# Attention by half blocks: tiles of 2 heads × 64 queries against 192 keys, values' product in six narrow passes

## The chip, the cores and the metric

The kernel runs on one NeuronCore of a Trainium2 chip. The metric is the time of one execution on the device, in microseconds (us). A core has five engines with instruction queues of their own, which run beside each other and wait for each other by semaphores: TensorE (PE, matrix products; the loading of its weights is shown as PEld), VectorE (DVE), ScalarE (ACT), GpSimd (POOL) and SyncE (SP), which here issues every DMA transfer between memory (DRAM) and the on-chip buffers (SBUF). Matrix products land in PSUM, a small memory in eight banks.

## The reference, cut to what matters

One decoder block on 2048 tokens of width 1024: a projection to 7680 columns, a convolution branch, an attention branch, gates, two output projections and norms. The change concerns the attention: 16 query heads and 4 key heads of 64 dimensions, a window of 128 keys, and a sink term in the softmax.

```python
def sliding_window_attention(q, k, v, sinks):
    ...
    qb = q.reshape(B, nb, BLOCK, N_KV_HEADS, GROUP, HEAD_DIM)
    kb, vb = band(k), band(v)                     # previous block and this one: 256 keys
    scores = jnp.einsum("bnqhgd,bnkhd->bnhgqk", qb, kb).astype(jnp.float32) * (HEAD_DIM ** -0.5)
    ...
    rel = qi + BLOCK - kj
    in_window = (rel >= 0) & (rel < WINDOW)       # BLOCK = WINDOW = 128
    ...
    scores = jnp.where(mask[None, :, None, None], scores, jnp.float32(-1e30))
    m = jnp.maximum(jnp.max(scores, axis=-1, keepdims=True), sink)
    p = jnp.exp(scores - m)
    denom = jnp.sum(p, axis=-1, keepdims=True) + jnp.exp(sink - m)
    probs = (p / denom).astype(v.dtype)
    out = jnp.einsum("bnhgqk,bnkhd->bnqhgd", probs, vb)
    return out.reshape(B, S, ATTN_WIDTH)
```

Each query sees exactly 128 keys. Of the 256 that a block of 128 queries is multiplied with, half are masked.

## The kernel before

**Numbers.** Every float32 operand of a large product is split into a high part (rounded to the format that TensorE takes in one pass, F32R) and a low part (the rest). A product is three passes: high·high, high·low, low·high. `put_split` and `split_lo` make the parts, on ACT and on DVE or POOL. The weights' low parts (`wlo`) are computed in the first sweep, stored to memory (`d_lo`), and read back in the second.

**Stages.** There are two sweeps (`s`) of 1024 tokens, each in eight blocks of 128. A sweep projects the GLU inputs, keys, values and queries, then the gates (`mm_ag`, `mm_cg`, `mm_ma`, `mm_mc`), then takes the two output projections (`mm_ya`, `mm_yc`) and the last product (`o`). A projection item is 48 passes of 512 columns, 10.88 us. The convolution runs on DVE (L512), spread over the same stretch.

**Order.** TensorE's order is the order in which the Python code emits its instructions. `Line` keeps a planned time: `project` yields 0.2275 us a pass, and after each step `Line.spend` looks whether a step of a chain is due. Each of the 32 tiles of attention in a sweep (head group `g` of 4 heads, block `b`) is such a chain, `attention(n)`, started every `ATT_EVERY` = 13.8 planned us, in three steps:

1. scores (`sc`, L690): eight passes, 4 heads × 2 key parts, of 256 key columns (128 in the very first block); then the copy to SBUF (L699), the predicated copy of the own block's half (L700), and the softmax (L704 to L715). As each query sees 128 keys, the two key blocks are folded into 128 slots: a slot holds the key of the own block up to the diagonal, and the previous block's after it;
2. after `LAT[0]` = 22 planned us: four transposes (`tpp`, L720) and the split of the result (`pt`, L725 and L248), and on POOL a masked copy of both parts (`pc`, L731);
3. after `LAT[1]` = 16: the values' product (`ov`, L740), four passes of 512 columns: `pt`, high and low, with the previous block's values `vt`, and `pc`, high and low, with the difference of the blocks' values `vd`. The output is scaled by a gate and stored to `d_a`.

`sc` takes two and `tpp` and `ov` one each of three PSUM banks (`tp`), in turn: a tile's scores need the bank that the transposes before them filled, and wait for the split of `pt` (DVE, L248).

Other engines' order, and that of the DMAs on SP, is set by a scheduler from priorities. SP issues in order and a DMA that waits holds up those behind it. In a sweep a round `r` of four projects the queries of one head of each group (`q_a`, `q_b`), rotates them, splits them and stores them to `d_q` (L605), two halves of 512 tokens each; `load_qk` brings a tile's queries and keys (L663, L667).

Of the kernel before, what the change touches and what calls it, by code (L numbers as in the profile page):

```python
# [19 lines left out]
P = 128  # L20
# [27 lines left out]
LAT = (22.0, 16.0)  # L48
# [5 lines left out]
def hybrid_block(ctx: ExitStack, tc: tile.TileContext, x, xt, par_d, w_in, w_conv, sinks, w_attn, w_out,  # L54
# [69 lines left out]
    causal_i = causal.bitcast(I32).unsqueeze(1).broadcast_to([P, 2, P])  # L124
# [7 lines left out]
    def load_sinks():  # L132
        nc.sync.dma_start(out=sink_bc, in_=sinks.partition_broadcast(P).rearrange("p o h -> p (o h)"))
        dve.tensor_scalar(out=nsink, in0=sink_bc, scalar1=-1.0, scalar2=None, op0=ALU.mult)
# [21 lines left out]
    d_q = dram.tile([2, 2, P, S // P, GQ, P], F32, name="d_q")  # L156
    d_k = dram.tile([2, 2, P, S], F32, name="d_k")

    d_a = dram.tile([NSWEEP * KC, P, 2, T], F32, name="d_a")
    v_halo = const.tile([P, NKV, 2, HD], F32R, name="v_halo")  # L160
# [328 lines left out]
    def sweep(s):  # L489
# [84 lines left out]
        def rope_items(name, e, store):  # L574
# [7 lines left out]
            def ev_b(half, ps):  # L582
# [6 lines left out]
                for i in range(2):  # L589
                    hl = slot(next_of("hl", AT[7:11]), [P, 2, TH], F32R, f"hl{s}_{name}_{half}_{i}")  # L590
                    put_split(hl, a[:, i, :], dve)
                    store(i, half, f(hl))
# [4 lines left out]
        def store_k(i, half, hl):  # L597
            t0 = s * T + half * TH
            nc.sync.dma_start(out=d_k[:, i, :, t0:t0 + TH].rearrange("a p t -> p a t"), in_=hl)

        def store_q(r):
            def store(i, half, hl):
                b0 = s * NB + 4 * half
                for a in range(2):
                    nc.sync.dma_start(out=d_q[a, i, :, b0:b0 + 4, r, :],  # L605
                                      in_=hl[:, a, :].rearrange("p (b t) -> p b t", t=P))

            return store


        vt, vd = {}, {}

        def v_item(i):
            def chain(half, vs):
# [8 lines left out]
                act.copy(v_last[:, i], vf[:, 3])  # L623
                for j in range(2):
                    bp = 2 * half + j
                    if i == 0:
                        vt[bp] = slot(AT[bp], [P, 2, NKV, 2 * HD], F32R, f"vt{s}_{bp}")
                        vd[bp] = slot((AT[15:] + X[1:] + X[:1])[bp], [P, 2, NKV, 2 * HD], F32R, f"vd{s}_{bp}")
                    for full, to in ((tp, vt), (d, vd)):
                        part = full[:, 2 * j:2 * j + 2, :].rearrange("p b (g d) -> p b g d", d=HD)  # L630
                        hi, lo = (to[bp][:, :, 2 * i:2 * i + 2, a * HD:(a + 1) * HD] for a in range(2))
                        act.copy(hi, part)
                        split_lo(lo, part, hi, dve)
# [16 lines left out]

        done, qk = {}, {}

        def load_qk(n):
# [5 lines left out]
            q, k = t[:, 0, :].rearrange("p (r t) -> p r t", t=P), t[:, 1, :].rearrange("p (a t) -> p a t", a=2)  # L659
            qk[n] = (q, k)  # L660
            fs = slice(g * HH, (g + 1) * HH)
            for i in range(4):
                nc.sync.dma_start(out=f(q[i * HH:(i + 1) * HH]), in_=d_q[i // 2, i % 2, fs, blk, :, :])  # L663
# [8 lines left out]
        def attention(n):  # L672
# [8 lines left out]
            for h in range(GQ):  # L681
                if h % 2 == 0:
                    scs.append(tp_ps.tile([P, 2, 2, P], F32, tag="tp", name=f"sc{u}_{h // 2}"))
                sc = scs[-1][:, h % 2]
                for j in range(2):
                    if first:
                        o, r = sc[:, 1, :], k[:, j, P:]
                    else:
                        o, r = sc, k[:, j]
                    pe.matmul(out=o, lhsT=q[:, h, :], rhs=r, start=(j == 0), stop=(j == 1))  # L690
# [5 lines left out]
            for i, sc in enumerate(scs):  # L696
                part = sb[:, 2 * i:2 * i + 2, :]
                if not first:
                    act.copy(part, sc[:, :, 0, :])  # L699
                dve.copy_predicated(out=part, mask=causal_i, data=sc[:, :, 1, :])  # L700
# [15 lines left out]
            yield 0.96, LAT[0]  # L716
# [7 lines left out]
            pt = slot(next_of("pt", AT[7:9]), [P, 2, GQ, P], F32R, f"pt{u}")  # L724
            act.copy(pt[:, 0], tpp)  # L725
            split_lo(pt[:, 1], tpp, pt[:, 0], dve)
            if first:
                seq = [(v_of(g, b), pt)]
            else:
                pc = slot(next_of("pc", AT[9:11]), [P, 2, GQ, P], F32R, f"pc{u}")  # L730
                pool.affine_select(out=pc, in_=f(pt), pattern=[[0, 2], [0, GQ], [1, P]],  # L731
                                   compare_op=ALU.is_ge, fill=0.0, base=0, channel_multiplier=-1)
                seq = [(v_of(g, b - 1), pt), (vd[b // 2][:, b % 2, g, :], pc)]
            yield 0.44, LAT[1]

            ov = tp_ps.tile([P, GQ, P], F32, tag="tp", name=f"ov{u}")
            nm = 2 * len(seq)
            for i in range(nm):
                vv, pp = seq[i // 2]
                pe.matmul(out=ov, lhsT=vv, rhs=pp[:, i % 2], start=(i == 0), stop=(i == nm - 1))  # L740
            ovp = ov.rearrange("p (i r) q -> p i r q", r=2)
            for r, own, other in ((0, slice(0, HD), slice(HD, P)), (1, slice(HD, P), slice(0, HD))):
                act.copy(oT[own], ovp[other, :, r, :])
                dve.tensor_tensor(out=oT[own], in0=ovp[own, :, r, :], in1=oT[own], op=ALU.add)
# [10 lines left out]
            yield nm * MM_US, 0.0  # L755

        def start_attention():
            load_qk(0)
            for n in range(NKV * NB):
# [367 lines left out]
```

## Time and profile before

| what | us |
|---|---|
| median of 3 runs | 2013.75 (2013.27 to 2015.22) |
| the profiled execution | 2013.65 |
| its span, first to last instruction | 2011.9 |
| PE busy | 1993.2 |
| DVE / ACT / POOL busy | 1346.4 / 1032.0 / 394.7 |
| mean granted clock of TensorE | 0.999 of full speed |

A row of groups reads: line, engine, operation, out<-in, shape, how often | busy us, mean ns of one | idle time of the engine before it and what ended it. A row of the timeline reads: start, duration, engine, line, operation, how often [idle time before it <- what ended it]; the duration of a matrix product holds its run through the array and overlaps the next, so its pace is seen from starts. A row of waits reads: who <- for whom: us in total, times, longest. A row of stretches reads: from:to, length, then the busy us of PE, PEld, DVE, ACT and POOL with counts, clock, DMA share and GB/s.

### The profile page before, as it was taken

The page shows a single profiled execution, that of the slowest core. Times are in us where ns is not written, and L with a number is a line of the kernel's source. Part 1 is how long each engine was busy: PE and PEld are TensorE (multiplying, and loading weights), DVE is VectorE, ACT ScalarE, POOL GpSimd, SP SyncE. Part 2 cuts the span into 40 slices and gives each one's busy share as a digit, 9 for nine tenths or more (in the row PEclk, how much of TensorE's full clock was granted, in tenths as well). Part 3 has the DMA queues.
Part 4 walks back from the last instruction along what each step waited for, and adds up shares of the span by engine and source line. Part 5 has one row for each costly group of instructions (what it writes and reads, how often), then busy time and mean ns, then how long its engine had stood idle before and what let it go on. Part 6 is the DMA issues. An engine that isn't in the chain of part 4 may idle for free.

```text
span 2011.9 us, 27257 instructions
## 1 busy us (share of the span) xinstructions
PE 1993.2 (99%) x9136; PEld 1655.4 (82%) x9136; DVE 1346.4 (67%) x1934; ACT 1032.0 (51%) x2270; POOL 394.7 (20%) x328
## 2 busy tenths in 40 slices
PE   8999999999999999999999999999999999999998
PEld 7888888887888888888888888888888888888887
DVE  6999679988996265123858669699888824431324
ACT  8322677667777354123523126777777764621222
POOL 0444332333232213241001120111011100001200
PEclk9999999999999999999999999999999999999999
DMA  8445655545556847445634556555545677564422
GB/s 306 147 143 175 225 166 171 166 155 169 168 172 216 263 171 247 146 156 214 218 117 159 160 175 194 166 175 176 175 153 171 181 229 262 175 227 141 157 110 84
DMA packets 268843, 361.13 MB, mean 180 GB/s; under 512 B 28576, under 2 KB 127008, under 8 KB 268704
## 3 DMA queue, kind: packets, MB, share of 16 engines
q1 hardware_dynamic: 268704, 359.40, 54.9%
q8 instruction: 72, 1.18, 0.2%
q14 instruction: 67, 0.55, 0.1%
HBM read 239.75 MB, written 119.54 MB: 179 GB/s over the span
## 4 chain that ended last, share of the span: by engine, by line
PE 88%; DVE 8%; DMA 1%; issue 1%; ACT 1%; SPq 0%; POOL 0%; ACTq 0%; DVEq 0%; POOLq 0%
PE o L1050 9%; PE mm_ya L286 9%; PE mm_yc L286 9%; PE mm_ga L286 8%; PE mm_gb L286 8%; PE mm_mc L286 7%; PE mm_ma L286 7%; PE mm_ag L286 6%; PE mm_cg L286 6%; DVE acc L512 5%; PE mm_q_a L286 4%; PE mm_q_b L286 4%; PE sc L690 2%; PE mm_v L286 2%; PE ov L740 2%
## 5 line engine op out<-in xcount | busy, mean ns | idle before, releaser
L512 DVE SCALAR_TENSOR_TENSOR acc<-glu,par,acc 128x1024 f32<-128x1024 f32 x464 | 595.9, 1284 | 5.9
L1050 PE MATMUL o<-wo,mT 128*128 128x512 f32 x768 | 174.8, 389 | 0.0
L1050 PEld LDWEIGHTS o<-wo,mT 128*128 128x128 f32 x768 | 144.1, 188 | 30.0
L286 PE MATMUL mm_ma<-hT,whi_ma 128*128 128x512 f32 x512 | 159.7, 393 | 0.0
L286 PE MATMUL mm_cg<-hT,whi_cg 128*128 128x512 f32 x512 | 159.7, 393 | 0.0
L286 PE MATMUL mm_ag<-hT,whi_ag 128*128 128x512 f32 x512 | 159.4, 392 | 0.0
L286 PE MATMUL mm_mc<-hT,whi_mc 128*128 128x512 f32 x512 | 157.9, 390 | 0.0
L286 PE MATMUL mm_ya<-aT,whi_ya 128*128 128x512 f32 x512 | 157.7, 389 | 0.0
L286 PE MATMUL mm_yc<-uT,whi_yc 128*128 128x512 f32 x512 | 157.7, 389 | 0.0
L731 POOL TENSOR_SCALAR_AFFINE_SELECT pc<-pt 128x1024 fp32r<-128x1024 f32 x60 | 65.6, 1094 | 431.8 <-DVE pt L248 431.8
L286 PE MATMUL mm_gb<-hT,whi_gb 128*128 128x512 f32 x448 | 139.4, 392 | 0.0
L286 PE MATMUL mm_ga<-hT,whi_ga 128*128 128x512 f32 x448 | 139.3, 392 | 0.0
L286 PEld LDWEIGHTS mm_ya<-aT,whi_ya 128*128 128x128 f32 x512 | 96.1, 188 | 20.0
L286 PEld LDWEIGHTS mm_yc<-uT,whi_yc 128*128 128x128 f32 x512 | 96.1, 188 | 19.9
L286 PEld LDWEIGHTS mm_mc<-hT,whi_mc 128*128 128x128 f32 x512 | 95.9, 188 | 20.0
L286 PEld LDWEIGHTS mm_ag<-hT,whi_ag 128*128 128x128 f32 x512 | 94.3, 188 | 18.4
L286 PEld LDWEIGHTS mm_cg<-hT,whi_cg 128*128 128x128 f32 x512 | 94.0, 188 | 18.2
L286 PEld LDWEIGHTS mm_ma<-hT,whi_ma 128*128 128x128 f32 x512 | 94.0, 188 | 18.1
L710 ACT ACTIVATE ss<-ss,st 128x128 f32<-128x128 f32 x256 | 99.7, 390 | 13.5 <-DVE st L705 12.7
L286 PE MATMUL mm_cg<-hT,wlo_cg 128*128 128x512 f32 x256 | 99.9, 390 | 0.0
L286 PE MATMUL mm_ma<-hT,wlo_ma 128*128 128x512 f32 x256 | 99.9, 390 | 0.0
L286 PE MATMUL mm_ag<-hT,wlo_ag 128*128 128x512 f32 x256 | 99.9, 390 | 0.0
(467 smaller groups left out, 4261.1 us busy)
## 6 DMA issues: line engine op xcount, KB each, us to landing
qk<-d_q SPq DMA_DIRECT2D x256, 64.0 KB, 2.2
d_a<-ss SPq DMA_DIRECT2D x128, 128.0 KB, 1.9
aT<-d_a SPq DMA_DIRECT2D x32, 512.0 KB, 5.7
qk<-d_k SPq DMA_DIRECT2D x240, 64.0 KB, 2.0
raw_ag<-in_w_in_dram SPq DMA_DIRECT2D x32, 256.0 KB, 3.7
d_ag<-ag SPq DMA_DIRECT2D x32, 256.0 KB, 2.2
ss<-d_ag SPq DMA_DIRECT2D x64, 128.0 KB, 2.6
raw_cg<-in_w_in_dram SPq DMA_DIRECT2D x32, 256.0 KB, 3.3
```

The costliest lines, as they stand in the source:

```text
L286: pe.matmul(out=ps, lhsT=a, rhs=b, start=(k == 0 and i == 0), stop=(k == KC - 1 and i == 2))
L512: dve.scalar_tensor_tensor(out=to, in0=glu[c][:, j:j + T], scalar=tap(c, j), in1=acc[c], op0=ALU.mult, op1=ALU.add)
L690: pe.matmul(out=o, lhsT=q[:, h, :], rhs=r, start=(j == 0), stop=(j == 1))
L710: act.activation(out=sb[:, h, :], in_=sb[:, h, :], func=AF.Exp, scale=SCALE, bias=ngm[:, h:h + 1], accum_out=den[:, h:h + 1])
L731: pool.affine_select(out=pc, in_=f(pt), pattern=[[0, 2], [0, GQ], [1, P]], compare_op=ALU.is_ge, fill=0.0, base=0, channel_multiplier=-1)
L740: pe.matmul(out=ov, lhsT=vv, rhs=pp[:, i % 2], start=(i == 0), stop=(i == nm - 1))
L1050: pe.matmul(out=ps, lhsT=a[:, c0:c0 + P], rhs=r, start=(k == 0 and i == 0), stop=(k == KC - 1 and i == 2))
```

## The change

A tile of attention is cut the other way. Before, a score tile had one head's 128 queries in its rows; now it has 64 queries (half a block, `qh`) of two heads. Such queries see no more than 192 keys, so a pass takes 192 columns, with as many passes as before. The slots are folded as before: the first 128 columns are copied, the last 64 go over the first 64 slots under a triangle `tri`. Queries lie in memory by half blocks and pairs of heads; a round with an even `r` splits into half of a tile, the next fills the other half, and both are stored together.

The values' product is done for the two halves of the queries apart, three passes of 256 columns each: `pt` high and low with the values that the half's slots hold before the mask (for the block's first half `vt` of the previous block; for its second `vm`, in the code `mix`: the previous block's last 64 values and this block's first 64), and one pass with the masked part. `pc` has the high part in 64 rows and the low part in the other 64, and the difference of values (`va`, `vb`) lies twice, in both halves of the rows. These tiles are made by writing values and differences to memory (`d_v`) and reading them back, six DMAs per head group and sweep (`load_v`): for the first group before attention starts, for the next when the last values' product of a group has been emitted, into the same buffers X[0] to X[2].

`LAT[0]` is 19 instead of 22; the planned times are 0.90 for scores (0.96 before) and 0.72 for values (0.91); the split of `pt` has a higher priority. The diff, cut to its core:

```diff
-LAT = (22.0, 16.0)
+LAT = (19.0, 16.0)
...
-        def store_q(r):
-            def store(i, half, hl):
-                b0 = s * NB + 4 * half
-                for a in range(2):
-                    nc.sync.dma_start(out=d_q[a, i, :, b0:b0 + 4, r, :],
-                                      in_=hl[:, a, :].rearrange("p (b t) -> p b t", t=P))
+        def store_q(r):
+            def store(i, half, src):
+                n = 2 * i + half
+                if r % 2 == 0:
+                    pair[n] = [slot(tags[n], [P, 2 * NB // 2, 2, HD], F32R, f"hq{s}_{r}_{n}_{tags[n]}")
+                               for tags in (AT[7:11], C[2:6])]
+                hi, lo = (t[:, :, r % 2, :] for t in pair[n])
+                src = src.rearrange("p (b t) -> p b t", t=HD)
+                act.copy(hi, src)
+                split_lo(lo, src, hi, dve)
+                if r % 2:
+                    b0 = s * 2 * NB + NB * half
+                    for a in range(2):
+                        nc.sync.dma_start(out=d_q[a, i, :, b0:b0 + NB, r // 2, :],
+                                          in_=f(pair[n][a]).rearrange("p b h t -> p b (h t)"))
...
+        def load_v(g):
+            mix, da, db = (slot(X[n], [P, NB, P], F32R, f"v{'mab'[n]}{s}_{g}") for n in range(3))
+            vg[0] = (mix, da, db)
+            lo_rows, hi_rows = slice(0, HD), slice(HD, P)
...
+            nc.sync.dma_start(out=f(mix[lo_rows, n0:]),
+                              in_=d_v[b0 + n0 - 1:b0 + NB - 1, hi_rows, 0, g].rearrange("b p d -> p b d"))
+            load(mix, 0, hi_rows, lo_rows, 0)
+            for at in (lo_rows, hi_rows):
+                load(da, 0, at, lo_rows, 1)
+                load(db, 0, at, hi_rows, 1)
...
-            for h in range(GQ):
...
-                    pe.matmul(out=o, lhsT=q[:, h, :], rhs=r, start=(j == 0), stop=(j == 1))
+            for qh in range(2):
+                scs.append(tp_ps.tile([P, 2, 2 * P], F32, tag="tp", name=f"sc{u}_{qh}"))
+                c0 = (P - HD * qh) if first else 0
+                for hp in range(2):
+                    w = q[:, 2 * qh + hp, :]
+                    for j in range(2):
+                        pe.matmul(out=scs[qh][:, hp, c0:3 * HD], lhsT=w,
+                                  rhs=k[:, j, qh * HD + c0:qh * HD + 3 * HD], start=(j == 0), stop=(j == 1))
...
-                dve.copy_predicated(out=part, mask=causal_i, data=sc[:, :, 1, :])
+                dve.copy_predicated(out=part[:, :, 0:HD], mask=tri_i, data=sc[:, :, P:3 * HD])
...
+            for a in range(2):
+                at = slice(a * HD, (a + 1) * HD)
+                pool.affine_select(out=pc[at], in_=f(pt[0:HD, a]), pattern=[[0, 2 * GQ], [1, HD]],
                                    compare_op=ALU.is_ge, fill=0.0, base=0, channel_multiplier=-1)
-                seq = [(v_of(g, b - 1), pt), (vd[b // 2][:, b % 2, g, :], pc)]
...
+            for qh in range(2):
+                cols = slice(qh * 2 * P, (qh + 1) * 2 * P)
+                seq = [] if first and not qh else [((v_of(g, b - 1), mix)[qh], pt[:, a, cols]) for a in range(2)]
+                seq.append(((da, db)[qh], pc[:, cols]))
+                for i, (vv, pp) in enumerate(seq):
+                    pe.matmul(out=ov[:, cols], lhsT=vv, rhs=pp, start=(i == 0), stop=(i == len(seq) - 1))
+            if b == NB - 1 and g + 1 < NKV:
+                load_v(g + 1)
```

What it does to TensorE's order is seen at the values' product of the first sweep's fifth block (`ov0_0_4`: sweep, group, block; `x4` stands for four passes). Before:

```order
L286 MATMUL mm_ag0_51_2799<-hT0_1_1_537,whi_ag0_50_2608 128x512 x2
L286 MATMUL mm_ag0_51_2799<-hT0_1_1_537,wlo_ag0_50_2609 128x512
L740 MATMUL ov0_0_4_2808<-pt0_0_4_2642,vt0_1_716 128x512 x2
L740 MATMUL ov0_0_4_2808<-pc0_0_4_2645,vd0_2_761 128x512 x2
L286 MATMUL mm_ag0_51_2799<-hT0_1_2_538,whi_ag0_50_2608 128x512 x2
L286 MATMUL mm_ag0_51_2799<-hT0_1_2_538,wlo_ag0_50_2609 128x512
L690 MATMUL sc0_0_7_0_2834<-qk0_7_2680 128x256 x4
L690 MATMUL sc0_0_7_1_2839<-qk0_7_2680 128x256 x4
```

After, at the same place:

```order
L791 MATMUL ov0_0_4_2807<-pt0_0_4_2645,vt0_1_722 128x256 x2
L791 MATMUL ov0_0_4_2807<-pc0_0_4_2648,va0_0_1701 128x256
L791 MATMUL ov0_0_4_2807<-pt0_0_4_2645,vm0_0_1700 128x256 x2
L791 MATMUL ov0_0_4_2807<-pc0_0_4_2648,vb0_0_1702 128x256
L292 MATMUL mm_ag0_50_2774<-hT0_0_6_460,whi_ag0_51_2630 128x512 x2
L292 MATMUL mm_ag0_50_2774<-hT0_0_6_460,wlo_ag0_51_2631 128x512
```

The next scores (`sc0_0_7`) followed after 3 projection passes and now follow after 18. Most tiles had 0 to 3 there and now have 15 to 18; between scores and the next transposes stand 24 projection passes instead of 36, and 12 between transposes and values as before.

SP's queue is seen in the second sweep, where the queries of round 1 are stored (`hl1_q1` before, `hq1_0` now: it holds rounds 0 and 1) and the low halves of the weights for the queries of round 2 are read. Before:

```order
L605 DMA d_q_107<-hl1_q1__0_0_10153 128x4x128
L605 DMA d_q_107<-hl1_q1__0_1_10158 128x4x128
L605 DMA d_q_107<-hl1_q1__0_0_10153 128x4x128
L605 DMA d_q_107<-hl1_q1__0_1_10158 128x4x128
L265 DMA wlo_q2_b10_10207<-d_lo_113 128x512
L265 DMA wlo_q2_b11_10213<-d_lo_113 128x512
L262 DMA raw_q3_b10_10372<-in_w_in_dram 128x512
L605 DMA d_q_107<-hl1_q1__1_0_10195 128x4x128
L605 DMA d_q_107<-hl1_q1__1_1_10200 128x4x128
```

After:

```order
L622 DMA d_q_110<-hq1_0_0_h7_9991 128x8x128
L622 DMA d_q_110<-hq1_0_0_c2_9992 128x8x128
L622 DMA d_q_110<-hq1_0_2_a9_9995 128x8x128
L622 DMA d_q_110<-hq1_0_2_c4_9996 128x8x128
L622 DMA d_q_110<-hq1_0_1_a8_10031 128x8x128
L622 DMA d_q_110<-hq1_0_1_c3_10032 128x8x128
L622 DMA d_q_110<-hq1_0_3_a10_10035 128x8x128
L622 DMA d_q_110<-hq1_0_3_c5_10036 128x8x128
L271 DMA wlo_q2_b10_10344<-d_lo_117 128x512
```

The stores of both halves, each twice as large, now stand ahead of that read. At round 3 it is the same with `wlo_ga`, and in the first sweep with the first tile's queries and keys.

More of the change, by code (lines that the diff above doesn't have):

```diff
@@ L123, in hybrid_block @@
                        base=0, channel_multiplier=1)
-    causal_i = causal.bitcast(I32).unsqueeze(1).broadcast_to([P, 2, P])
+    tri = const.tile([P, HD], F32, name="tri")
+    for u in range(2):
+        us = slice(u * HD, (u + 1) * HD)
+        pool.tensor_copy(out=tri[us], in_=causal[us, us])
+    tri_i = tri.bitcast(I32).unsqueeze(1).broadcast_to([P, 2, HD])
     eps = const.tile([P, 2], F32, name="eps_t")
@@ L132, in load_sinks @@
     def load_sinks():
[L133 removed]
+        for u in range(2):
+            nc.sync.dma_start(out=sink_bc[u * HD:(u + 1) * HD], in_=sinks[u].partition_broadcast(HD))
         dve.tensor_scalar(out=nsink, in0=sink_bc, scalar1=-1.0, scalar2=None, op0=ALU.mult)
@@ L623, in chain @@
                 act.copy(v_last[:, i], vf[:, 3])
+                g2 = slice(2 * i, 2 * i + 2)
+                vd = slot(next_of(f"vd{s}", AT[15:] + X[1:]), [P, 4, 2, 2 * HD], F32R, f"vd{s}_{i}_{half}")
+                part = d.rearrange("p b (g d) -> p b g d", d=HD)
+                hi, lo = (vd[:, :, :, a * HD:(a + 1) * HD] for a in range(2))
+                act.copy(hi, part)
+                split_lo(lo, part, hi, dve)
+                b0 = s * NB + 4 * half
                 for j in range(2):
@@ L627, in chain @@
                         vt[bp] = slot(AT[bp], [P, 2, NKV, 2 * HD], F32R, f"vt{s}_{bp}")
[L628 to L633, printed above, removed]
+                    part = tp[:, 2 * j:2 * j + 2, :].rearrange("p b (g d) -> p b g d", d=HD)
+                    hi, lo = (vt[bp][:, :, g2, a * HD:(a + 1) * HD] for a in range(2))
+                    act.copy(hi, part)
+                    split_lo(lo, part, hi, dve)
+                    nc.sync.dma_start(out=d_v[b0 + 2 * j:b0 + 2 * j + 2, :, 0, g2].rearrange("b p g d -> p b g d"),
+                                      in_=f(vt[bp][:, :, g2]))
+                nc.sync.dma_start(out=d_v[b0:b0 + 4, :, 1, g2].rearrange("b p g d -> p b g d"), in_=f(vd))
                 yield 0.44, 0.0
@@ L723, in attention @@
             nc.sync.dma_start(out=ga, in_=spill["ag"][e2, :, qs].rearrange("c p q -> p c q"))
[L724 to L731, printed above, removed]
+            pt = slot(next_of("pt", AT[7:9]), [P, 2, TH], F32R, f"pt{u}")
@@ L734, in attention @@
             yield 0.44, LAT[1]
[L736 to L741, printed above, removed]
+            ov = tp_ps.tile([P, TH], F32, tag="tp", name=f"ov{u}")
+            mix, da, db = (t[:, b, :] for t in vg[0])
+            for qh in range(2):
[4 more added lines that the diff above has]
+                    pe.matmul(out=ov[:, cols], lhsT=vv, rhs=pp, start=(i == 0), stop=(i == len(seq) - 1))
```

63 lines of the change are left out of this document (38 added, 25 removed).

## The prediction

> **What bounds the kernel.** I read the page first: the line of the busiest engine and the first line of the chain that ended last.
>
> ```profile
> PE 1993.2 (99%) x9136; PEld 1655.4 (82%) x9136; DVE 1346.4 (67%) x1934; ACT 1032.0 (51%) x2270; POOL 394.7 (20%) x328
> PE 88%; DVE 8%; DMA 1%; issue 1%; ACT 1%; SPq 0%; POOL 0%; ACTq 0%; DVEq 0%; POOLq 0%
> ```
>
> TensorE (PE) has work in 99% of the span, in an order written out in the program. So the time is the sum of its passes plus its waits, and each is to be counted. A busy share does not say how densely passes follow each other, so next come the groups by shape for what there is, and the timeline for the pace, from the start of one row to the start of the next.
>
> ```profile
> L690 PE MATMUL sc<-qk 128*128 128x256 f32 x480 | 68.8, 284 | 6.0 <-DVE pt L248 5.9
> L740 PE MATMUL ov<-pt,vt 128*128 128x512 f32 x120 | 37.0, 389 | 0.0
> L740 PE MATMUL ov<-pc,vd 128*128 128x512 f32 x120 | 36.9, 389 | 0.0
> L690 PE MATMUL sc<-qk 128*128 128x128 f32 x32 | 4.0, 268 | 0.0
> ```
>
> ```profile
> 208.60 1.00 PE L690 MATMUL sc<-qk 128*128 128x128 f32 x8
> 209.44 0.69 PE L286 MATMUL mm_ga<-hT,whi_ga 128*128 128x512 f32 x2
> ...
> 304.18 0.62 PE L740 MATMUL ov<-pt,vt 128*128 128x512 f32 x2
> 304.63 0.62 PE L740 MATMUL ov<-pc,vd 128*128 128x512 f32 x2
> 305.09 0.61 PE L286 MATMUL mm_ag<-hT,whi_ag 128*128 128x512 f32 x2
> ...
> 305.77 1.11 PE L690 MATMUL sc<-qk 128*128 128x256 f32 x8
> 306.72 0.63 PE L286 MATMUL mm_ag<-hT,whi_ag 128*128 128x512 f32 x2
> ```
>
> A mean of 389 ns is the life of one pass; four passes of 512 columns take 305.09 − 304.18 = 0.91 us, 0.227 each. Eight passes of 256 columns take 0.95 us (0.119 each), and eight of 128 take 0.84 (0.105 each). So a pass of 128 columns costs nearly as much as one of 256: it has a floor that columns do not set. Next, where PE waits, and one such wait in the timeline.
>
> ```profile
> PE sc L690 <- DVE pt L248: 5.9, 6, 2.5
> PE mm_gb L286 <- ACT u_c L353: 5.5, 1, 5.5
> ```
>
> ```profile
> 346.86 0.63 PE L690 MATMUL sc<-qk 128*128 128x256 f32 x4
> 348.31 0.68 DVE L248 TENSOR_TENSOR pt<-tpp,pt 128x512 fp32r<-128x512 f32 x1
> 349.05 0.54 PEld L690 LDWEIGHTS sc<-qk 128*128 128x128 f32 x4 [1.76 <-DVE pt L248]
> ```
>
> Six times the second half of a tile's scores waits until VectorE has split the transposed probabilities (pt) and so freed a PSUM bank. The other wait is in the opening and stays.
>
> **The change, part by part.** The sum is made against the profiled execution: 2013.65 us, span 2011.9; the median of the runs, 2013.75, is 0.1 above it.
>
> Scores. In 60 of 64 tiles eight passes shrink from 256 to 192 columns. Ends: 0.95 us a tile if narrowing brings nothing, 0.84 if the floor holds at 192 too. Streamed at the pace of the wide passes 192 columns take 0.227 × 192/512 = 0.085 us, below the floor of 0.105, so I take 0.86, near the lower end. 60 × (0.95 − 0.86) = 5.4 us less (0 to 6.6). The four first blocks are at the floor before and after: nothing.
> [...]
>
> Values. Four passes of 512 columns become six of 256, because both parts of the masked probabilities now stand in one operand. From 0.91 to 6 × 0.119 = 0.71: 60 × 0.20 = 12.0 us less. Ends: 0.68 if a pass is half a wide one (13.8 less), 0.78 if passes cost 0.13 (7.8 less); I take the row with the same number of columns. First blocks go from two wide passes to four narrow: 4 × 0.03 = 0.1 more.
>
> The order. The transposes come after 24 projection passes instead of 36, and 15 to 18 passes stand between values and next scores instead of 0 to 3. The bank that the scores wait for thus has some 3.4 us more, over the longest wait of 2.5: the 5.9 us go, and with them the refill (349.05 is 1.71 after the earlier four passes were through, not 1.56), about 0.9 in six times: 6.8 less (0 to 7.5). What is late next is the softmax, which loses 3 us:
>
> ```profile
> 345.69 1.27 ACT L715 ACTIVATE ss<-ss,st 128x128 f32<-128x128 f32 x4
> ...
> 357.82 0.60 PE L720 MATMUL tpp<-ident_r,ss 128*128 128x128 f32 x4
> ...
> 362.26 1.09 POOL L731 TENSOR_SCALAR_AFFINE_SELECT pc<-pt 128x1024 fp32r<-128x1024 f32 x1 [4.32 <-DVE pt L248]
> ...
> 374.50 0.62 PE L740 MATMUL ov<-pt,vt 128*128 128x512 f32 x2
> ```
>
> This tile's probabilities are ready 357.82 − 346.96 = 10.9 us before their transposes; 7.9 remain: nothing. The mask (pc) ends 11.1 us before the values' product. It becomes two operations of half the partitions and half the elements: between 1.1 us and 2.2 in all, hidden either way. The predicated copy has half the columns and the split of pt a higher priority; both ease VectorE, and PE does not see it.
>
> Queries. Before, each of four rounds r stores its own parts, four stores of 256 KB per half; now rounds 0 and 2 store nothing, and 1 and 3 store both rounds: 4 × 128 × 8 × 128 × 4 B = 2.10 MB per half. All DMAs stand in one queue on SyncE (SP), and what is issued behind that burst waits for it. In sweep 1 the low halves of weights, which before stood between the two halves' stores, now stand behind all eight:
>
> ```profile
> 1141.75 0.37 SPq L605 DMA_DIRECT2D d_q<-hl_q__0_0_10153  x1
> ...
> 1144.61 1.76 SPq L265 DMA_DIRECT2D wlo_q_b<-d_lo  x2
> ...
> 1147.61 0.37 SPq L605 DMA_DIRECT2D d_q<-hl_q__1_0_10195  x1
> ...
> 1149.87 0.50 SPq L605 DMA_DIRECT2D d_q<-hl_q__1_1_10200  x1
> ...
> 1155.22 0.39 PE L286 MATMUL mm_q_b<-hT,wlo_q_b 128*128 128x512 f32 x1
> ```
>
> ```profile
> 1188.50 1.52 SPq L605 DMA_DIRECT2D d_q<-hl_q__0_0_10487  x2
> ...
> 1191.29 2.26 SPq L265 DMA_DIRECT2D wlo_ga<-d_lo  x2
> ...
> 1195.13 1.73 SPq L605 DMA_DIRECT2D d_q<-hl_q__1_1_10534  x2
> ...
> 1198.74 0.39 PE L286 MATMUL mm_ga<-hT,wlo_ga 128*128 128x512 f32 x1
> ```
>
> How fast the engines drain such stores, in a stretch full of them (the last two numbers are the DMA share and GB/s), and how long a small transfer takes in an empty queue:
>
> ```profile
> 1195.50:1199.00 3.50, 3.50 (x18) 2.88 (x17) 0.00 (x0) 1.32 (x3) 0.00 (x0) 1.00 0.99 299
> DMA to landing us min/median/max: 1.9/2.0/2.2
> ```
>
> 2.10 MB at 299 GB/s is 7.0 us. First burst: from 1141.75, with 1.5 of start (the 1.9 less the transfer itself), the first half ends at 1150.3. The second is issued from 1147.61 to 1149.87, so it follows without a gap and ends at 1157.3. The weights' 256 KB add 0.9 and 0.4 to land: 1158.6, while PE wants them at 1155.22: 3.4 us of wait. Second burst, all 3.4 later: 1191.9 + 1.5 + 7.0 + 7.0 + 1.3 = 1208.7 against 1202.1: 6.6 us. In sweep 0 the first tile's queries and keys stand behind the burst:
>
> ```profile
> 191.55 0.38 SPq L605 DMA_DIRECT2D d_q<-hl_q__0_0_1633  x1
> ...
> 200.52 0.55 SPq L605 DMA_DIRECT2D d_q<-hl_q__1_1_1680  x1
> ...
> 203.60 0.43 SPq L667 DMA_DIRECT2D qk<-d_k  x1
> ```
>
> 191.55 + 1.5 + 14.0 = 207.1, 0.5 to land the burst, and 2.0 for the keys behind it: 209.6 against the scores at 208.60: 1.0 us. Together 11.0 more. The ends: 0 if the weights find another way past, 20 if the vector work behind the stores is late by 3 us each time.
>
> Values' tiles. Row-doubled tiles go to memory and come back per group of heads: 8.4 MB out and 12.6 in, 21 MB on top of 361.
>
> ```profile
> q1 hardware_dynamic: 268704, 359.40, 54.9%
> ```
>
> That share becomes some 58%. A group's tiles lie in one set of buffers: the six loads (1.57 MB, 5.3 us at 299 GB/s) can start only after the last values' product of the group before, and must land before the next, 51 projection passes, scores, transposes and products later, 51 × 0.227 + 0.86 + 0.35 + 0.71 = 13.5 us. With 2.5 us to issue six (0.42 each, the keys' row) and 1.5 to start they are there after 9.3 at the latest: nothing, end up to 4 us at each of six changes.
>
> Sum: −5.4 − 12.0 + 0.1 − 6.8 + 11.0 = −13.1, so 2013.65 − 13.1 = 2000.6, and 2000.7 against the median.
>
> **Rivals.**
> The bursts are hidden. For it: in sweep 0 the weights have no low halves to read, and PE waited for no transfer in the run before. Against: 1158.6 and 1208.7 above. Without the 11.0: 1989.6.
> The bursts cost more, or values' tiles come late at some changes of group: 5 to 10 us more, 2006 to 2010. For it: loads on SP stand behind a store that waits for GpSimd; against: 4 us of room.
> Slower: values' tiles come late at every change. SP issues in order, and if it hangs on an unfinished store for over 4.2 us past the product, PE waits. Six changes at 4 us, 24 in all, give 2025; from 2.2 us at each the gain is gone. Against it: no row has PE waiting for SP now.
> Columns alone set the pace of a pass: then scores take 8 × 0.085 = 0.68 and values 0.68: 60 × (0.18 + 0.03) = 12.6 less, 1988. The rows of 0.84 and 0.95 speak against it.
> [...]
> Narrow passes bring nothing (0.95 and 0.78 a tile): 9.7 back, 2010, no change. Only 0.119 at 256 columns speaks on this, against it.
>
> **How the numbers follow.** Forecast (1994 to 2006) 0.55; bursts hidden 0.20; more waits 0.13, a third of it above 2009.7; slower 0.05; columns alone 0.04; nothing from narrowing 0.03. 0.2% is 4 us, about what a measurement can tell from no change: the limits are 2009.7 and 2017.8. Faster: 0.55 + 0.20 + 0.09 + 0.04, and 0.01 of the last = 0.89; the same 0.06; slower 0.05. The range from 1988 to 2009 leaves out some 0.12, and takes in both ends of the bursts.
>
> **What would show it.** Right: scores' passes at 0.105 to 0.110 and values' at about 0.119 from start to start; no wait of sc for pt; waits of PE of 3 to 7 us for wlo_q_b and wlo_ga in sweep 1, once each, and about 1 us at the first scores of sweep 0. Wrong: tpp waiting for ss, ov for the row-doubled tiles, or passes of 192 columns as long as those of 256.

## The result, and the profile after

The changed kernel takes 2064.60 us (median of 4 runs, 2062.71 to 2065.92) against 2014.49 for the kernel before on the same chip (2013.27 to 2015.92): a ratio of 1.025, 95% interval 1.023 to 1.027. It is 50 us slower. The forecast was 13 us faster, range 1988 to 2009.

The profiled execution took 2065.01 us, its span 2063.3 (before 2011.9), at a mean granted clock of 0.991 (before 0.999). The page's line of busy engines, the first two lines of its chain and its line on the DMA queue:

```profile
PE 2001.2 (97%) x9264; PEld 1660.7 (80%) x9264; DVE 1330.4 (64%) x1930; ACT 1014.6 (49%) x2263; POOL 417.3 (20%) x398
PE 56%; DVE 20%; ACT 8%; DMA 3%; issue 2%; SPq 1%; POOL 0%; ACTq 0%; DVEq 0%; POOLq 0%
DVE acc L518 12%; PE o L1105 8%; PE mm_ya L292 8%; PE mm_yc L292 8%; PE mm_mc L292 7%; PE mm_ma L292 6%; PE mm_ga L292 4%; PE mm_gb L292 3%; PE mm_q_b L292 2%; PE mm_q_a L292 2%; ACT ss L758 2%; PE mm_cg L292 2%; DVE ss L798 1%; DVE st L752 1%; ACT L758 1%
q1 hardware_dynamic: 301872, 380.25, 58.1%
```

VectorE (DVE) has less work than before and yet holds 20% of the chain, where it held 8%; the largest piece is the convolution (`acc`, L518). The waits of PE, longest in total first:

```profile
PE sc L735 <- DVE pt L254: 19.6, 21, 2.2
PE tpp L768 <- DVE ss L798: 6.6, 5, 2.2
PE mm_gb L292 <- ACT u_c L359: 5.3, 1, 5.3
PE mm_ma L292 <- DMA wlo_ma<-d_lo: 4.5, 1, 4.5
PE mm_ga L292 <- DMA wlo_ga<-d_lo: 4.4, 1, 4.4
PE mm_cg L292 <- DMA wlo_cg<-d_lo: 4.1, 2, 3.2
PE mm_q_b L292 <- DMA wlo_q_b<-d_lo: 4.0, 1, 4.0
PE sc L735 <- DMA qk<-d_k: 2.7, 1, 2.7
PE ov L791 <- DMA vb<-d_v: 2.2, 4, 1.1
```

With two smaller rows they come to 55 us, 12 before. The forecast's burst waits are there (wlo_q_b, wlo_ga, the keys). The wait of sc for pt, which was to vanish, is three times as long, and transposes now wait for the evacuation of values (`tpp <- ss`).

The pace of the narrow passes is the forecast one. Scores of a tile that waits for nothing, and a values' product, in the timeline of PE:

```profile
1655.76 1.03 PE L735 MATMUL sc<-qk 128*128 128x192 f32 x8
1656.63 0.65 PE L292 MATMUL mm_ma<-hT,whi_ma 128*128 128x512 f32 x2
...
276.15 0.40 PE L791 MATMUL ov<-pt,vt 128*128 128x256 f32 x2
276.38 0.28 PE L791 MATMUL ov<-pc,va 128*128 128x256 f32 x1
276.50 0.40 PE L791 MATMUL ov<-pt,vm 128*128 128x256 f32 x2
276.74 0.28 PE L791 MATMUL ov<-pc,vb 128*128 128x256 f32 x1
276.86 0.40 PE L292 MATMUL mm_gb<-hT,whi_gb 128*128 128x512 f32 x1
```

Eight passes of 192 columns take 0.87 us (0.109 each), six of 256 take 0.71 (0.118).

How VectorE makes PE wait is seen in one stretch of 20 us: first the timeline of VectorE, then of ScalarE (ACT), then of PE.

```profile
1262.65 0.68 DVE L752 TENSOR_REDUCE st<-ss 128x4 f32<-128x512 f32 x1
1263.25 1.28 DVE L518 SCALAR_TENSOR_TENSOR acc<-glu,par,acc 128x1024 f32<-128x1024 f32 x1
...
1265.89 2.62 DVE L518 SCALAR_TENSOR_TENSOR acc<-glu,par,acc 128x1024 f32<-128x1024 f32 x2
...
1277.08 1.28 DVE L518 SCALAR_TENSOR_TENSOR acc<-glu,par,acc 128x1024 f32<-128x1024 f32 x1
1278.28 0.68 DVE L752 TENSOR_REDUCE st<-ss 128x4 f32<-128x512 f32 x1
1278.87 1.28 DVE L518 SCALAR_TENSOR_TENSOR acc<-glu,par,acc 128x1024 f32<-128x1024 f32 x1
1280.06 0.15 DVE L753 SCALAR_TENSOR_TENSOR st<-st,nsink 128x4 f32<-128x4 f32 x1
```

```profile
1273.20 0.64 ACT L269 CAST whi_gb<-raw_gb 128x512 fp32r<-128x512 f32 x1
1280.29 1.28 ACT L758 ACT_TABLE_LOAD   x1 [6.45 <-DVE st L753]
1281.59 0.40 ACT L758 ACTIVATE ss<-ss,st 128x128 f32<-128x128 f32 x1
...
1281.99 0.56 ACT L775 CAST pt<-tpp 128x512 fp32r<-128x512 f32 x1
```

```profile
1274.30 0.60 PE L768 MATMUL tpp<-ident_r,ss 128*128 128x128 f32 x4
...
1281.63 0.58 PE L735 MATMUL sc<-qk 128*128 128x192 f32 x4
1283.45 0.69 PE L735 MATMUL sc<-qk 128*128 128x192 f32 x4 [1.24 <-DVE pt L254]
```

From one tile's maximum (L752 at 1262.65) to the next (1278.28) VectorE needs 15.6 us, since 11 instructions of the convolution stand between them; PE's tile is planned at 13.8. ScalarE, whose queue keeps the program's order, stands 6.45 us before the exponentials of the new tile. The transposes of the tile before were done at 1274.9, but their copy (pt, L775) is queued behind the first of those exponentials and starts at 1281.99; VectorE's split follows at 1282.71, and the third bank is free at 1283.4, when the second half of the next scores has waited 1.24 us.

The number of convolution instructions between one maximum and the next, counted in the traces over sweep 0's tiles 1 to 15:

```
before  4  8  9  8  2  0  7  7  8  8  1  9  7  9  6
after   5 10 10  6  0  0  9  7  9  6  4  8 10  9  0
```

A channel has 31 of them in both (4 + 8 + 9 + 8 + 2, and 5 + 10 + 10 + 6), and all channels the same number. A list scheduler sets their places, and with the narrow tiles it lets a channel's 31 run in denser groups. Ten of them and the tile's other instructions on VectorE (4.3 us in this trace: L748, L752, the four small steps, L254 twice, L798 twice, L799) are 10 x 1.28 + 4.3 = 17.1 us, 3.3 over PE's tile; tiles of eight to ten follow each other in twos and threes. By the same sum the eight and nine of the kernel before are 0.7 and 2.0 over, which e16 takes up.

In the mean of the 64 tiles the maximum ends 3.3 us after the last score pass in the kernel before and 7.3 us in the changed one. The split of pt, which frees the bank, ends 2.8 us after the last transpose in the kernel before and 6.4 us in the changed one.

The table load in the second fence is new in one respect. These are the groups of ScalarE's loads ahead of the exponentials, first before (L710), then after (L758); the last part is the idle time just ahead of them:

```profile
L710 ACT ACT_TABLE_LOAD x55 | 70.6, 1283 | 2.4 <-issue 1.4
```

```profile
L758 ACT ACT_TABLE_LOAD x57 | 73.1, 1283 | 142.0 <-DVE st L753 142.0
```

Before, the load itself waited for nothing (2.4 us of idle time in 55), and what was left of the maximum could end during its 1.28 us; now the load stands behind the wait, and its time comes on top. The built programs say why: the predicated copy takes only 64 of the 128 columns that ScalarE copied, so an exponential reads columns whose last writer is ScalarE itself. The exponential then waits for its own engine, and the wait for VectorE is an instruction of its own ahead of the table load, in 53 of 57 places (in the kernel before in 3 of 55).

### The profile page after: what moved, and what is told of

It is laid out like the page before. It is cut to its first block, busy times and chain, and to the rows that moved or that the text cites. A ratio compares the mean times of both kernels' runs of the same rounds, so it can differ in the third digit from the quotient of the medians.

```text
span 2063.3 us, 27786 instructions
## 1 busy us (share of the span) xinstructions
PE 2001.2 (97%) x9264; PEld 1660.7 (80%) x9264; DVE 1330.4 (64%) x1930; ACT 1014.6 (49%) x2263; POOL 417.3 (20%) x398
## 4 chain that ended last, share of the span: by engine, by line
PE 56%; DVE 20%; ACT 8%; DMA 3%; issue 2%; SPq 1%; POOL 0%; ACTq 0%; DVEq 0%; POOLq 0%
DVE acc L518 12%; PE o L1105 8%; PE mm_ya L292 8%; PE mm_yc L292 8%; PE mm_mc L292 7%; PE mm_ma L292 6%; PE mm_ga L292 4%; PE mm_gb L292 3%; PE mm_q_b L292 2%; PE mm_q_a L292 2%; ACT ss L758 2%; PE mm_cg L292 2%; DVE ss L798 1%; DVE st L752 1%; ACT L758 1%
## 5 line engine op out<-in xcount | busy, mean ns | idle before, releaser
L518 DVE SCALAR_TENSOR_TENSOR acc<-glu,par,acc 128x1024 f32<-128x1024 f32 x464 | 595.4, 1283 | 4.2
L780 POOL TENSOR_SCALAR_AFFINE_SELECT pc<-pt 64x512 fp32r<-64x512 f32 x128 | 83.6, 653 | 552.9 <-ACT pt L775 522.1
L798 DVE TENSOR_TENSOR ss<-ov,ss 64x256 f32<-64x256 f32 x128 | 53.7, 419 | 85.9 <-ACT ss L797 84.2
```

The costliest lines, as they stand in the source:

```text
L518: dve.scalar_tensor_tensor(out=to, in0=glu[c][:, j:j + T], scalar=tap(c, j), in1=acc[c], op0=ALU.mult, op1=ALU.add)
L780: pool.affine_select(out=pc[at], in_=f(pt[0:HD, a]), pattern=[[0, 2 * GQ], [1, HD]], compare_op=ALU.is_ge, fill=0.0, base=0, channel_multi ...
L798: dve.tensor_tensor(out=to, in0=ovp[own, :, r], in1=to, op=ALU.add)
```

## The experiments

**e1, e2, e3: order of the passes, priority.**

```diff
e1  -LAT = (19.0, 16.0)      e3, in the kernel before:  -LAT = (22.0, 16.0)
    +LAT = (22.0, 16.0)                                 +LAT = (19.0, 16.0)
e2  -with tc.high_priority(offset=4 * PRIO):   # around pt's copy and split
```

> The changed kernel with the planner's latency of the softmax back at 22.0 us, nothing else: 36 to 39 projection passes stand again between a tile's scores and the transposes of the tile before, and 0 to 3 between values and next scores. Theory A (the order): with only 24 passes in between, the copy of the transposes (pt) comes to ScalarE while it is still at the exponentials of the tile whose scores were just made, so pt is done 6 to 10 us after the transposes and holds the third bank. Then the waits of sc for pt (19.6 us) and of tpp for the evacuation of ov (6.6) fall to 6 us or less together, and the slow passes behind the two longest of them go too: 2035 us (2030 to 2042). Theory B (the raised priority of pt did it) and theory C (the transfers on SyncE did it): the waits stay within 5 us of 26, 2060 to 2066.

> The changed kernel with pt copied and split at the priority of the kernel before. Theory B (the raised priority reorders ScalarE and VectorE to the harm of the scores' evacuation): waits of sc and tpp fall from 26 us to under 10, 2040 us. Theory A: the priority helps or does nothing, the waits are 20 to 35 us and the time 2060 to 2072.

> The kernel before with the planner's latency of the softmax at 19.0 us, nothing else: 24 passes between scores and transposes, 12 to 15 between values and next scores. Theory A: PE now waits for pt and for the evacuation of ov as in the changed kernel, 15 to 30 us in place of 5.9: 2025 to 2040 us. The mechanism of the prediction (the bank that the scores wait for has 3.4 us more): the 5.9 us go, 2007 us. Theories B and C: no change or the prediction's 2007.

e1 took 2068.55 us (ratio to before 1.027, 1.026 to 1.029), e2 2070.37 (1.028, 1.026 to 1.030), e3 2005.37 (0.996, 0.994 to 0.997). Theories A and B fall: with the old order sc waits 34.6 us for pt, without the priority 39.0, both longer than the 26.2 of the changed kernel's first two rows. In e3 the prediction's own mechanism holds: the opening's is the one wait of PE left.

```profile
PE mm_gb L286 <- ACT u_c L353: 5.4, 1, 5.4
```

So the moved order is good for 9 us in the kernel before, and the loss comes from something that meets it in the changed one.

**e4: value tiles loaded once per sweep.**

```diff
-            if b == NB - 1 and g + 1 < NKV:
-                load_v(g + 1)
```

> The changed kernel in which groups of heads 1 to 3 go on using group 0's row-doubled value tiles, so 18 of 24 loads of them per sweep are left out (their values are those of another group; every pass and every other transfer stays). Theory C (SyncE hangs on the unfinished product at a change of group, and the low halves of weights behind it come late): the waits for wlo_ma (4.5) and wlo_cg (4.1) and of ov for its tiles (2.2) go, with some 18 passes at half pace behind them (4 us): 2050 us (2046 to 2054); the waits of sc and tpp stay near 26. Theory A alone: the waits for wlo have another cause and stay, 2060 to 2066.

2060.04 us (1.023, 1.021 to 1.024): 4.6 less, under half of what was expected. The waits for wlo_ma and wlo_cg are gone (10.8 us with those of ov), but those of sc and tpp grew from 26.2 to 33.9. PE gains at one place and waits at the next: here removed waits did not add up.

**e5: score passes of 256 columns.**

```diff
-  pe.matmul(out=scs[qh][:, hp, c0:3 * HD], lhsT=w, rhs=k[:, j, qh * HD + c0:qh * HD + 3 * HD], ...)
+  pe.matmul(out=scs[qh][:, hp, 0:4 * HD], lhsT=w, rhs=k[:, j], ...)     # not in first blocks
```

> The changed kernel whose score passes stay 256 columns wide (64 further columns of the same keys, written beside the 192 and read by nothing); the order of instructions on ScalarE and VectorE, which comes from a list scheduler, moves with it: between a tile's score copies and its exponentials stand 1.9 other instructions on ScalarE in the mean, 1.3 in the changed kernel, 2.4 in e3. Theory D (order on the two engines): ScalarE waits for VectorE's maximum with nothing else in between (142 us in the changed kernel, L758), so both engines fall behind PE; with more in between, the waits of sc and tpp (26 us) fall to 15 or less and the time, with 60 x 0.08 = 5 us more of passes, is about 2050 (2045 to 2058). Theory E (the two engines have too much work between one tile and the next, whatever the order): the waits stay within 6 us of 26 and the time is 2064 to 2070.

2029.55 us (1.008, 1.006 to 1.009): 35 less, although PE has 5 us more of passes (0.953 a tile again). In the second half of queries the pass starts 64 keys early here, so its values differ; its length does not. The waits of sc and tpp fall to 0.2 and 0.7. The order matters, and more than was expected; but this edit moves the passes and the order together. Between maxima stand mostly 7 to 9 convolution instructions in this program.

**e6, e7: less work on VectorE.**

```diff
e6  -for j in range(1, TAPS):
    +for j in range(2, TAPS, 2):       # an empty step in each other's place
e7  -dve.tensor_tensor(out=oT, in0=oT, in1=ga, op=ALU.mult)
    +pool.tensor_tensor(out=oT, in0=oT, in1=ga, op=ALU.mult)
    -split_lo(hl[:, 1].bitcast(F32R), oT, hl[:, 0], dve)
    +split_lo(hl[:, 1].bitcast(F32R), oT, hl[:, 0], pool)
```

> The changed kernel with every second tap of the depthwise convolution left out (its values differ): some 240 of 464 VectorE instructions of 1.28 us go, about 3.5 us of each tile's 13.8. Theories D and E both have VectorE's instructions between the scores and the exponentials as the cause: the waits of sc for pt and of tpp for ov's evacuation go to under 4 us, with the refills and slow passes behind them (9 us): 2030 us (2024 to 2036). What is left over 2000.7 is then what the transfers cost. If the waits have another source (transfers, the ring of three banks itself): over 15 us of them stay, above 2045.

> The changed kernel with the last two steps of a tile's evacuation, the product with the gate and the split into high and low part, on GpSimd in place of VectorE: 0.85 us less on VectorE per tile, and two hand-overs between ScalarE and VectorE less. Theory E: the waits of sc and tpp fall from 26 to 12 or less, 2045 us (2038 to 2052). Theory D: the exponentials still stand right behind the score copies; the waits fall by 8 at most, 2055 to 2066. Slower than 2066 if GpSimd's instructions slow VectorE's.

e6 took 2030.64 us (1.008, 1.007 to 1.010), as expected: the convolution is what VectorE is late with. The waits are less clean than expected: 6.7 us of that for pt are left in place of under 4, and that for wlo_ma grew from 4.5 to 10.7. e7 took 2061.57 (1.023, 1.022 to 1.025), with 23.0 of 26.2 us of waits left: 0.85 us less in a tile helps little where ten times 1.28 stand in a row. Theory E in its plain form falls.

**e8: queries stored in every round.**

```diff
-  if r % 2:
-      nc.sync.dma_start(out=d_q[a, i, :, b0:b0 + NB, r // 2, :], in_=f(pair[n][a])...)
+  rs = slice((r % 2) * HD, (r % 2 + 1) * HD)
+  nc.sync.dma_start(out=d_q[a, i, :, b0:b0 + NB, r // 2, rs], in_=f(pair[n][a][:, :, r % 2, :]))
```

> The changed kernel in which every round of queries stores its own part at once, as in the kernel before: the same bytes in runs of 256 in place of 512, eight stores of 256 KB per half in all four rounds. The prediction's theory of the bursts: the waits for wlo_q_b (4.0), wlo_ga (4.4) and of the first scores for their keys (2.7) go, and the 26 passes at half pace behind them (5.9 us): 2048 us (2044 to 2052). Rival: short runs drain at half the rate, so the queue is as late in every round: the waits stay or grow, 2060 to 2075.

2049.02 us (1.017, 1.016 to 1.019): 15.6 less, as expected. The waits for wlo_q_b and for the keys are gone, that for wlo_ga is 1.5 in place of 4.4. TensorE, VectorE, ScalarE and GpSimd keep their order in this run, row for row, so the difference is that of the stores. The bursts are real, and cost more than their 11.1 us of waits (below, the clock).

**e9, e10, e11: the table load.**

```diff
e9   -dve.copy_predicated(out=part[:, :, 0:HD], mask=tri_i, data=sc[:, :, P:3 * HD])
     +dve.copy_predicated(out=part, mask=tri_i,          # tri_i: zero in the upper 64 columns
     +                    data=sc[:, :, P:3 * HD].unsqueeze(2).broadcast_to([P, 2, 2, HD]))
e10  as e9, with out=part.rearrange("p h (u t) -> p h u t", t=HD)
e11, in the kernel before:
     -dve.copy_predicated(out=part, mask=causal_i, data=sc[:, :, 1, :])
     +dve.copy_predicated(out=part[:, :, 0:HD], mask=causal_i[:, :, 0:HD], data=sc[:, :, 1, 0:HD])
```

> The changed kernel whose predicated copy again overwrites all 128 columns that ScalarE copied from the scores (the mask is zero in the upper 64), as in the kernel before. Then the exponentials' newest input is VectorE's alone, and in the built program the load of ScalarE's table ahead of them (1.28 us) carries no wait in 57 of 57 places; in the changed kernel it waits for VectorE's maximum in 53 of 57, in the kernel before in 3 of 55. Theory F (the table load has moved behind the wait, into the chain of every tile): ScalarE's idle time at the load falls from 142 us to under 30, the waits of sc and tpp from 26 to under 5, and 2028 us (2020 to 2036). Theory D (order): the order on both engines is that of the changed kernel to within a few rows, so the waits stay at 20 to 30 and the time at 2060 to 2070.

> The same as e9 with the output of the predicated copy written with one more dimension (2 x 64 columns in place of 128): the same elements, the same order of all instructions, but the table loads carry the wait again in 53 of 57 places. Theory F: as the changed kernel, 2060 to 2072. If the width of the predicated copy itself makes the difference, it is as fast as e9.

> The kernel before, whose predicated copy takes only the first 64 of its 128 columns (the others keep the copied scores, so values differ): less work on VectorE, and the table loads now carry the wait in 57 of 58 places; passes, stores and loads are those of the kernel before. Theory F: the waits of sc for pt grow from 5.9 to 20 to 40 us: 2030 to 2050 us. If only the narrow passes, the stores or the values' tiles do harm: 2008 to 2016.

e9 took 2052.76 us (1.019, 1.017 to 1.021), e10 2065.22 (1.025, 1.023 to 1.027), e11 2009.04 (0.997, 0.996 to 0.998). e9 and e10 have the same instructions in the same order; the row of the load and the longest wait of PE, in e9 and in e10:

```profile
L766 ACT ACT_TABLE_LOAD x57 | 73.1, 1283 | 1.0
...
PE sc L739 <- DVE pt L258: 25.0, 18, 4.1
```

```profile
L766 ACT ACT_TABLE_LOAD x57 | 73.1, 1283 | 156.4 <-DVE st L761 156.4
...
PE sc L739 <- DVE pt L258: 32.9, 27, 4.5
```

The load behind its wait costs 12.5 us, a third of what theory F gave it. In e11 the load waits as well (48 us of idle time in 58), and the kernel is 6 us faster than before (2014.99 beside it), far from theory F's 2030 to 2050: VectorE has less to copy, and PE's waits for pt fall from 5.9 to 2.3. Where VectorE is in time, the load costs less: e11 gained 6 us although its load waits. Theory F is a part and not the cause.

**e12: everything so far, with GpSimd loading the value tiles.**

```diff
 e8's and e9's edits, and in load_v, six times:
-  nc.sync.dma_start(...)
+  nc.gpsimd.dma_start(...)
```

> The changed kernel with e9's predicated copy, e8's stores of queries in every round, and the loads of row-doubled value tiles issued by GpSimd, so that SyncE no longer stands still at a change of group. Theory F with the bursts and the value tiles as the rest: 2028 less 16 (bursts) less 8 (waits for wlo_ma, wlo_cg and their slow passes): 2003 us (1995 to 2010). If GpSimd's loads come late for the products: up to 2025.

2050.56 us (1.018, 1.017 to 1.020), 48 over the expectation. PE waits 12.6 us for value tiles and 7.7 for the mask on GpSimd, where the loads are queued, and sc and tpp keep 15.8. Both the cause and the cure were missed.

**e13: the convolution spread over the tiles.** Each tile renews a copy of the taps after its maximum, so that the instructions handed out for it cannot be placed ahead of it.

```diff
+  tg = work.tile([P, TAPS], F32, tag="tg", name=f"tg{u}", bufs=4)
+  dve.tensor_copy(out=tg, in_=par[:, c, 0:TAPS])
+  dve.copy_predicated(out=tg, mask=mx[:, 0:1].bitcast(I32).broadcast_to([P, TAPS]), data=par[:, c, 0:TAPS])
+  taps_of[c] = tg                      # read by tap(c, j) from here on
```

> The changed kernel, in which each tile renews a small copy of the channel's taps after its maximum (two VectorE instructions of 31 elements) and the convolution's next instructions read that copy: so only those handed out for this tile can stand behind it, 5 or 6 between one maximum and the next in place of 10, 10, 6, 0, 0. Passes, stores, reloads, the table loads that wait (54 of 58) and all work stay. Theory G (bunching: ten instructions of 1.28 us and the tile's own 4.3 are 17 us, over the tile's 13.8, so VectorE falls behind by 3 us a tile while a channel lasts): the waits of sc and tpp fall from 26 us to under 5, 2030 us (2024 to 2036). If the narrow passes themselves or the ring of three banks make the waits, they stay over 15: 2050 to 2068.

2014.46 us (1.000, 0.999 to 1.001): 50 us less, 15 more than expected. The counts between maxima are 6 5 6 6 5 6 10 2 5 6 6 6 6 5 6 over the same 15 tiles. All waits of PE of 1 us or more:

```profile
PE mm_gb L298 <- ACT u_c L365: 5.6, 1, 5.6
PE mm_q_b L298 <- DMA wlo_q_b<-d_lo: 3.9, 1, 3.9
PE mm_ga L298 <- DMA wlo_ga<-d_lo: 3.9, 1, 3.9
PE mm_ma L298 <- DMA wlo_ma<-d_lo: 3.3, 1, 3.3
PE mm_cg L298 <- DMA wlo_cg<-d_lo: 2.2, 2, 1.2
PE sc L742 <- DVE pt L260: 1.0, 1, 1.0
```

PE's passes, in the same order row for row, the banks, the stores and the loads are those of the changed kernel, and VectorE has some 130 instructions more. The maximum now ends 2.5 us after the last score pass in the mean (7.3 in the changed kernel), the split of pt 3.5 us after the last transpose (6.4). So what made the kernel slower was where the convolution stands, together with what the scheduler moves along with it: about a quarter of the other rows of VectorE and of ScalarE change places too, and no run parts the two.

**e14, e15: with the other causes mended.**

```diff
e14  e13 with e8's and e9's edits
e15  e14, and after a group's last product:
     -load_v(g + 1)
     +line.soon.append(lambda: load_v(g + 1))     # three passes later, without the priority
```

> e13 with e9's predicated copy (table load ahead of its wait) and e8's stores in every round. If the causes add: 2030 less 15 for the bursts, and 0 to 4 for the table load, which is hidden once VectorE keeps up: 2013 us (2008 to 2018). If they were one cause seen three times: 2025 to 2030.

> e14 with the loads of the next group's value tiles handed out three passes after the last product of a group and without its priority, so that fewer of SyncE's other loads stand behind the wait for that product. If SyncE's standing still is what is left (waits for wlo_ma and wlo_cg, some 8 us with the slow passes behind them): 2005 us (2000 to 2010). If the loads of tiles then come late for the products themselves: 2013 to 2020.

e14 took 1993.52 us (0.990, 0.989 to 0.991): faster than both kernels by 20 and 71 us, and 20 under its own expectation of 2013. That counted from e13's expected 2030; from e13's measured 2014.46 it is 20.9 less, against the 15 to 19 expected. Without the bursts the prediction's sum is 1989.6, 4 below this run. Its waits and the first line of its chain:

```profile
PE mm_gb L302 <- ACT u_c L369: 6.8, 1, 6.8
PE mm_ma L302 <- DMA wlo_ma<-d_lo: 1.7, 1, 1.7
PE mm_ya L302 <- DVE mp L984: 0.8, 1, 0.8
...
PE 97%; DVE 2%; DMA 1%; ACT 0%; issue 0%; SPq 0%; DVEq 0%; ACTq 0%
```

e15 took 2031.86 (1.009, 1.008 to 1.011), with 25.8 us of waits of ov, 11.9 of them put down to value tiles by the table of waits and the rest to engines or to nothing seen. That is over the 2013 to 2020 expected for tiles that come late. Its theory falls; that the loads need their early place in SyncE's queue is the likely reading, but was not tested further.

**e16, e17: the same spread in the kernel before, and e14 without the freed table load.**

```diff
e16  e13's edit in the kernel before
e17  e14 without e9's edit
```

> The kernel before, its latency of 22.0 unchanged, with e13's copy of the taps: 5 or 6 convolution instructions behind each maximum in place of 7 to 9. Theory G: its 5.9 us of waits for pt have the same cause and go, with their refills: 2007 us (2005 to 2010). If they come from the order of the passes (the transposes only 0 to 3 passes ahead of the scores' second bank) they stay: 2012 to 2016.

> e14 without e9's predicated copy: the table loads wait for VectorE's maximum again in 54 of 58 places. If that load costs only where VectorE is late, as theory G has it: within 4 us of e14, 1994 to 1998. If it lies in every tile's chain whatever VectorE does: 12 us more than e14, 2003 to 2008.

e16 took 2005.76 us (0.996, 0.995 to 0.997); its wait of sc for pt is 1.0 in place of 5.9. So that wait had the same cause, and e3's shorter latency only gave it room. It also means that 8 of the 50 us that the spread brings in e13 were there to be had in the kernel before. e17 took 2000.32 (0.994, 0.993 to 0.995), 6.8 over e14: between the two theories. Of that difference 2.8 us are waits of PE (12.1 in all against 9.3); the rest was not traced.

## Why the prediction was wrong

- **The step that failed** is in "The order": "the 5.9 us go", with "7.9 remain: nothing" and "both ease VectorE, and PE does not see it" behind it. It gave the bank that scores wait for 3.4 us more and took the rest of the tile as it stood in the old program. But the split of pt, which frees that bank, ended 3.6 us later behind the transposes (6.4 in place of 2.8), which used up the 3.4, and the wait grew from 5.9 to 19.6 us. The step did not ask what else VectorE does between one tile and the next, nor whether those instructions keep their places. The page's mean for VectorE was 67%, but its busy tenths in 40 slices of the kernel before (line below) stood at 8 and 9 for most of the attention of sweep 0, slices 5 to 13. e13 puts the price of this step at 50 us against the forecast, and e13 and e16 together at some 42 between the two kernels. The counts of convolution instructions could have been read in the order of the built program beforehand. Transposes did wait for `ss`, one of the forecast's signs of being wrong, but for the evacuation of values into it and not for late probabilities.

```profile
DVE  6999679988996265123858669699888824431324
```

- **The mask edit** was costed at nothing as well. It moved a wait onto the table load: 12.5 us while VectorE lags (e9 against e10), 6.8 or less when it does not (e14 against e17).
- **Scores and values** were right: 60 x (0.953 - 0.871) = 4.9 us against 5.4, and 60 x (0.907 - 0.712) = 11.7 against 12.0.
- **The order's gain** of 6.8 was right as a mechanism, and alone is worth 9.1 (e3); in the changed kernel it had no room to act.
- **The bursts** were right in place and about right in size: waits of 4.0, 4.4 and 2.7 against 3.4, 6.6 and 1.0. That they are 11.1 in all against 11.0 is luck, as the three misses cancel. Their price is 14 to 16 us (e17 against e13, e8), since passes behind the longest waits ran at half pace, a term that the sum lacked.
- **Value tiles** at "nothing, end up to 4 us at each of six changes": 10.8 us of waits (wlo_ma, wlo_cg and ov), 10.3 of them in sweep 1, where low halves of weights stand behind these loads in SyncE's queue; without the reloads the kernel gains 4.6 in all (e4).
- **The rivals** had a chance of 0.05 for slower, by another mechanism. None had VectorE or ScalarE as the bound, although the fences already showed sc waiting for VectorE.

The sum of the changed kernel: passes 16.6 us less; starts of passes late by some 83 us in all (start to start, over the passes' normal pace), 18.5 before. That is some 48 of the 51.4 us between the two spans; the rest was not traced. What in the scheduler makes narrow scores pack the convolution more densely is not seen in any trace and stays open; e5 shows only that wide ones undo much of it.

## What to carry to other kernels

Where one engine's filler work shares an in-order queue with the chain of a tile, count the filler instructions between one tile's step and the next in the built program, before and after: with the same 31 in a channel, 5, 10, 10, 6 in place of 4, 8, 9, 8, 2 went with most of a loss of 50 us here. Tying each tile's share of the filler to the tile costs two small instructions a tile and brought more than the passes' savings. And a cheaper predicated copy can be dearer, if it leaves part of its target to another writer and so gives the reader a second wait: 12.5 us here while VectorE was late (e10 against e9).

## What the runs showed of the hardware

The clock: behind some waits PE's granted clock was halved, in the changed kernel's trace for 3.4 us four times and for 6.8 us three times before its end, in that of the kernel before never between its first 12 us and its end. These are stretches of the changed kernel, just behind the waits of 4.4 us at 1222 and of 2.2 at 544, and then one of the kernel before, behind its wait of 2.5 at 460 (the clock is the third number from the end):

```profile
1226.40:1230.40 4.00, 3.94 (x9) 3.14 (x10) 0.00 (x0) 0.00 (x0) 0.00 (x0) 0.50 0.71 187
546.00:550.00 4.00, 3.74 (x11) 3.17 (x12) 3.79 (x8) 3.83 (x9) 0.65 (x1) 0.57 0.56 190
```

```profile
463.00:466.00 3.00, 3.00 (x15) 2.58 (x16) 2.94 (x7) 0.74 (x2) 0.00 (x0) 1.00 0.22 68
```

The 64 wide passes that begin in these seven stretches took 0.43 us in the mean from start to start in place of 0.227, some 13 us more. The length of a wait alone does not decide: the wait of 2.2 us was followed by a halved stretch, that of 2.5 in the kernel before was not. By the trace's records of the granted clock the seven begin at 211.8, 546.3, 621.4, 1177.8, 1225.6, 1525.9 and 1635.2; from one to the next are 98, 22, 163, 14, 88 and 32 times 3.41 us, as on a fixed grid. In this trace each begins right behind a step of that grid in which PE stood for 1.9 us or more, and none begins behind a step with 1.8 or less. On the same grid that wait of 2.5 us lies across the edge of two steps, with 1.5 us at most in either. These are the numbers of two traces, and no run set a wait by itself.

In e8 the stores in runs of 256 bytes drained more slowly. These are stretches of a burst of stores, in the changed kernel (runs of 512) and in e8 (runs of 256):

```profile
1215.00:1219.00 4.00, 4.00 (x19) 3.30 (x19) 0.48 (x1) 0.90 (x2) 0.00 (x0) 1.00 0.96 285
```

```profile
1203.00:1206.00 3.00, 3.00 (x15) 2.49 (x14) 1.48 (x3) 0.68 (x2) 2.52 (x2) 1.00 0.87 217
```

That is 285 GB/s against 217, a quarter less in these two stretches, where the rival in e8's expectation had half. e8 won all the same, as each of its bursts has half the bytes: its stores of 256 KB land 3.7 us after their issue, the changed kernel's of 512 KB after 5.8.
